# Trunk of latent and linear attention: the value and gate projections of the linear attention done as seven quadrant products a block

## The chip, the cores and the metric

The kernel runs on one core of one Trainium2 chip. The metric is device time in microseconds (us), the median of three runs. The engines are named as the profile names them: PE multiplies matrices (PEld is its weight load), DVE works on vectors, ACT evaluates activations, POOL is the general engine, SP issues DMA transfers. ACT and POOL issue transfers too.

## The reference

Two layers over 512 tokens of width 1024, all in float32. Each layer is a mixer and a squared-ReLU MLP, both with RMS norm ahead and a residual add behind. The mixer of layer 0 is latent attention (MLA), that of layer 1 gated linear attention (GLA) with four heads of key width 128 and value width 256. The part that matters:

```python
def gla_mixer(xn, w_in, w_gk_up, b_gk, g_norm, w_o):
    h = xn @ w_in                      # 1024 -> 512 q, 512 k, 1024 v, 1024 g, 16 a
    gk = log_sigmoid(a @ w_gk_up + b_gk) / 16
    # chunked scan over 64 tokens: S <- decay * S + k^T v, o = q S + (q k^T decay) v
    o = rms_norm(o, g_norm)            # per head
    o = o * silu(g)
    return o @ w_o
```

## The kernel before

The residual stream is kept transposed in SBUF: `xT[j]` is 128 channels (one eighth of the width) by 512 tokens. The program runs MLA, MLP 0, GLA, MLP 1 and the final norm.

Precision: every float32 operand of a matmul is split into a rounded high part and the remainder. `split` (L124, L127) writes the high part (`wh` for weights) on ACT and the low part (`wl`) on DVE; `piece` does this for a weight tile of 128 x 1024. `mm3` (L132 to L134) then issues three matmuls for a product: high by high, high by low, low by high. The row names of the profile that say `L132`, `L133`, `L134` are these. The two MLPs already use a scheme with seven products instead of eight (Winograd's form of Strassen), from which come the lines L917 to L920 (sums of quadrants of x), L1048 and L1056 (sums of weight quadrants), L1060 and L1064 (sums of products in PSUM).

The GLA stage has five stretches on PE: a head (first q and k projections, gate products, L1372), the blocks v and g of heads 0 and 1, the second q and k projections with the states of heads 0 and 1, the blocks V and G of heads 2 and 3, and a tail (the last head's own and past products, the turning of the gated heads, the output projection).

A block is `b_type`: 1024 input channels, 512 output columns, all 512 tokens. It takes one weight half (128 x 4 x 512) per load, cuts it in two pieces, and for each of the 8 channel groups and 4 token tiles does one `mm3` with 512 columns. The finished token tile goes to `done`: for v, `v_done` writes a high part on ACT (L1360) and a low part on DVE (L1361), with the token's norm factor `rtok`; for g, `g_done` lets ACT compute Silu (L1283), whose table is loaded ahead, with the exponential's table loaded back after (L139).

The order is set by two Python generators. `proj` yields after each piece of projection work, `heads` after each step of the recurrence; a number `PACE` times the units that `proj` yields decides how many steps of `heads` come between. The tile framework keeps each engine's instructions in program order but for priorities, and an engine waits for what its next instruction needs. `levels` is the recurrence inside chunks (L1422 to L1471); `states`, `own_tiles` and `past` build state, in-chunk and inter-chunk outputs (L1549, L1556); `gated` multiplies by the gate (L1577, L1579); `gather` turns a gated head into the layout that the output projection reads, `Y` (L149, L1598, L1599). `out_start` begins the output projection for three of its eight output groups; `out_proj` ends it. Tiles come from tagged slots: `slot("B")` is a slot of 128 x 512 of which there are few, and a slot is free only when its last reader is done.

Of the kernel before, what the change touches and what calls it, by code (L numbers as in the profile page):

```python
# [50 lines left out]
def trunk_kernel(ctx: ExitStack, tc: tile.TileContext, t_in: dict, out: bass.AP):  # L51
# [57 lines left out]

    X_AT = 44  # L110
    both_room = []
# [45 lines left out]
    W_ROOM, W_AT = 1152, 128  # L157
    AT_UP = (124, 60)

# [3 lines left out]

    def piece(raw, a, n, order=lambda i: i, at=(W_AT, W_AT)):
        hi = room_for("wh", a, n, at[0])
        lo = room_for("wl", a, n, at[1])
        split(raw, hi, lo, order=order)
        return hi, lo
# [7 lines left out]

    gains = const.tile([P, N_GAIN + NT + 32], F32, name="gains")
    pos_i = gains[:, N_GAIN : N_GAIN + NT].bitcast(I32)
    invf = gains[:, N_GAIN + NT :]


    xall = const.tile([P, ND, S], F32, name="xT")
    xT = [xall[:, j] for j in range(ND)]
    x_in = t_in["x"].rearrange("(j p) t -> p j t", p=P)

    def load_x(q, j):
        q.dma_start(xall[:, j], x_in[:, j])

    eps_t = const.tile([P, 1], F32, name="eps_t")
    DVE.memset(eps_t, EPS)  # L190
    one_t = const.tile([P, 1], F32, name="one_t")
    DVE.memset(one_t, 1.0)
    ones_r = const.tile([P, P], F32R, name="ones128")
    ones128 = f(ones_r)
    DVE.memset(ones128, 1.0)
    ident_b = rk.tile([P, P], BF16, name="ident_b")
    DVE.tensor_copy(ident_b, ident)
# [51 lines left out]
    class Norm:  # L249
# [22 lines left out]
        def scaled(self, j, src, order=lambda i: i):  # L272
            parts = self.parts[j] = both_parts(j, X_AT if self.g == "mlp" else 0)
# [3 lines left out]
            DVE.scalar_tensor_tensor(lo, src, g, f(hi), ALU.mult, ALU.subtract)  # L277
            self.out[j] = (hi, lo)
# [551 lines left out]
    def mlp(layer, nrm, nxt=None):  # L830
# [15 lines left out]
        turn = [0]  # L846
        s5 = fast.tile([P, 2 * S], F32, tag="sum", name="sum5")

        def laid(t):
# [388 lines left out]
    def gla(layer, nrm, vtag, ytag):  # L1238
# [6 lines left out]

        def b_type(c0, hf, done):
            banks = [bank("b"), bank("b"), bank("b"), bank("ac"[hf])]

            def mms(w, kk, k, t):
                xk = cut(X[k], slice(None), slice(t * P, (t + 1) * P))  # L1250
                mm3(banks[t], xk, cut(w, slice(None), kk), k == 0, k == ND - 1)

            for kc in range(2):
                raw = load(
                    w_in[kc * 512 : (kc + 1) * 512, c0 + hf * 512 : c0 + hf * 512 + 512].rearrange("(k p) n -> p k n", p=P), 4, 512
                )
                for g in range(2):
                    w = piece(raw[:, 2 * g : 2 * g + 2], 2, 512)
                    k0 = kc * 4 + g * 2
                    if k0 + 2 < ND:  # L1260
                        for kk in range(2):
                            for t in range(NT):
                                mms(w, kk, k0 + kk, t)
                            yield
                    else:
                        for t in range(NT):
                            for kk in range(2):
                                mms(w, kk, k0 + kk, t)
                            done(t, banks[t])
                            if t % 2:  # L1270
                                yield

# [3 lines left out]
        def g_done(hf):  # L1276
            G[hf] = gp.tile([P, NT, 2, HV], F32, tag="g", bufs=1, name=f"g{hf}")

            def done(t, p):
                s = G[hf][:, t]  # L1280
                with tc.high_priority():
                    tc.keep_in_program_order(
                        ACT.activation(s.rearrange("p a b -> p (a b)"), p, AF.Silu, scale=rtok[:, t : t + 1])  # L1283
                    )
                    if t == NT - 1:
                        exp_set()
                if t == NT - 1:
                    gdone.add(hf)

            return done  # L1290
# [4 lines left out]
        def proj_qk(c):  # L1295
            raw = col_chunk(w_in, c * 256, 256)
            w = [piece(raw[:, :, j * P : (j + 1) * P], ND, P) for j in range(2)]
# [25 lines left out]
        DVE.tensor_tensor(own, nrm.rstd.rearrange("p (t c) -> p t c", t=NT), ident.unsqueeze(1).to_broadcast([P, NT, P]), ALU.mult)  # L1323
        rtok = sb.tile([P, NT], F32, tag="rtok", name="rtok")
        DVE.reduce_sum(rtok, own, AX.X)


# [25 lines left out]
        vdone, gdone = set(), set()  # L1353
        V = [[None, None] for _ in range(NT)]

        def v_done(hf):
            def done(t, p):
                hi, lo = slot(vtag), slot(vtag)
                r = rtok[:, t : t + 1]
                ACT.activation(hi, p, AF.Copy, scale=r)  # L1360
                DVE.scalar_tensor_tensor(lo, p, r, f(hi), ALU.mult, ALU.subtract)  # L1361
                V[t][hf] = (hi, lo)
                if t == NT - 1:
                    vdone.add(hf)

            return done
# [161 lines left out]
        def head_values(h):  # L1528
            vs = slice((h % 2) * HV, (h % 2 + 1) * HV)
            return [cut(V[j][h // 2], slice(None), vs) for j in range(NT)]  # L1530

# [38 lines left out]
        def gated(h):  # L1570
            at, hf = AT[h], h // 2
            at["ms"] = sb.tile([P, NT], F32, tag="gms", bufs=2, name=uname("gms"))
            for i in range(NT):
                if i % 2:
                    for r in (i - 1, i):
                        sq = tmp((P, HV))
                        ACT.activation(sq, at["o"][r], AF.Square, accum_out=at["ms"][:, r : r + 1])  # L1577
                        g = G[hf][:, r, h % 2, :]
                        DVE.tensor_tensor(g, at["o"][r], g, ALU.mult)  # L1579

        def head_norm(h):
            r = small_rstd(AT[h]["ms"], NT, 1.0 / HV)
            for i in range(NT):
                g = G[h // 2][:, i, h % 2, :]
                if i % 2:
# [4 lines left out]
        def gather(h):  # L1590
            hf = h // 2
            for c in range(2):
                p = bank("c")
                for i in range(NT):
                    tr(p[:, i * P : (i + 1) * P], G[hf][:, i, h % 2, c * P : (c + 1) * P])
                hi, lo = slot(ytag), slot(ytag)
                gn = gcol("gn", 2 * layer + c)
# [4 lines left out]
        def proj():  # L1602
            parts = {
                "v": lambda: b_type(2 * DK, 0, v_done(0)),
                "g": lambda: b_type(2 * DK + D, 0, g_done(0)),
                "q": lambda: proj_qk(1),
                "k": lambda: proj_qk(3),
                "V": lambda: b_type(2 * DK, 1, v_done(1)),
                "G": lambda: b_type(2 * DK + D, 1, g_done(1)),
            }  # L1610
            for c in "vgqkVG":
                for _ in parts[c]():
                    yield 2 if c in "qk" else 1


        def heads():
            for h in (0, 2):
# [35 lines left out]
                yield from run((gather, h))  # L1653
                if h:
                    begun[0][2](4)
                yield from run((gather, h + 1))

        begun = []
        gates(0)
        for _ in rest:  # L1660
# [22 lines left out]
    load_x(ACT, 1)  # L1683
    SP.dma_start(gains, t_in["gains"])
    load_part(1, 2)
# [47 lines left out]
    psum_layout(False)  # L1733
    slot_layout(SLOT_AT)
    Y, begun = gla(0, n_mix1, "B", "B")
    n_mlp1 = Norm(ND, inv_dr, "mlp", ND)
    out_proj(t_in["gla_w_o"][0], Y, n_mlp1, begun)


# [57 lines left out]
```

## Time and profile before

| | us |
|---|---|
| median of three runs (1039.48 to 1039.76) | 1039.68 |
| profiled execution | 1039.79 |
| its span in the profile | 1038.1 |
| PE busy | 1028.9 |
| DVE busy | 879.2 |
| ACT busy | 694.4 |
| POOL busy | 92.7 |

One execution is profiled; the span runs from its first to its last instruction. The stage of linear attention takes 220.6 us of it, from 495.9 to 716.5, and the table of stretches in the prediction divides that. Rows of groups give line, engine, operation, tiles with shapes, count, then busy time and the mean of one in ns, then the engine's idle time before them with what ended it. Rows of the timeline begin with the start in us and the duration in us.

### The profile page before, as it was taken

How to read it: one execution, taken by the hardware profiler on the slowest of the kernel's cores; microseconds unless marked ns; L12 is line 12 of the kernel's file. 1: busy time of each engine (PE TensorE's matmuls, PEld its weight loads, DVE VectorE, ACT ScalarE, POOL GpSimd, SP SyncE). 2: the span in 40 equal slices, each digit the busy share in tenths (PEclk: the TensorE clock that was granted, in tenths of full speed). 3: DMA queues.
4: the chain of work that ended last, by engine and by line, in shares of the span. 5: the costliest groups of instructions: out<-in, count | busy, mean ns of one | idle time of the engine just before them, and what ended most of it. 6: DMA issues, size and time to landing. Idle time of an engine off the chain costs nothing.

```text
span 1038.1 us, 16859 instructions
## 1 busy us (share of the span) xinstructions
PE 1028.9 (99%) x6522; PEld 923.0 (89%) x6522; DVE 879.2 (85%) x1343; ACT 694.4 (67%) x1130; POOL 92.7 (9%) x128
## 2 busy tenths in 40 slices
PE   9999999999999999999999999999999999999997
PEld 7788888899999999998888888888989989989986
DVE  7889976999989989989686399469799999898994
ACT  7667754676776776786445566565677687677784
POOL 7400000400001101000000000000000001100000
PEclk9999999999999999999999999999999999999999
DMA  7501214777677777623312222164568777777422
GB/s 230 127 22 41 73 50 140 205 194 207 189 198 209 169 205 200 157 84 122 90 42 85 91 69 75 48 165 148 144 196 201 189 196 201 192 193 186 121 82 82
DMA packets 63169, 145.85 MB, mean 140 GB/s; under 512 B 9488, under 2 KB 32016, under 8 KB 60528
## 3 DMA queue, kind: packets, MB, share of 16 engines
q1 hardware_dynamic: 52928, 113.57, 33.8%
q0 software_dynamic: 8064, 29.36, 16.4%
q10 hardware_dynamic: 2096, 1.84, 0.6%
q8 instruction: 51, 0.84, 0.3%
q14 instruction: 30, 0.25, 0.1%
HBM read 142.39 MB, written 2.10 MB: 139 GB/s over the span
## 4 chain that ended last, share of the span: by engine, by line
PE 92%; DVE 4%; ACT 2%; DMA 1%; issue 1%; ACTq 0%; SPq 0%; DVEq 0%
PE ps L987 25%; PE ps L1007 13%; PE ps L1000 13%; PE ps L132 10%; PE ps L133 10%; PE ps L134 10%; PE ps L1175 2%; PE ps L149 1%; PE ps L1429 1%; PE ps L1209 1%; PE ps L436 1%; PE ps L1556 1%; DVE wl L127 1%; ACT wh L124 1%; PE ps L1479 0%
## 5 line engine op out<-in xcount | busy, mean ns | idle before, releaser
L124 ACT ACTIVATE wh<-wraw 128x1024 fp32r<-128x1024 f32 x139 | 146.1, 1056 | 113.7 <-PE ps L133 38.4
L127 DVE TENSOR_TENSOR wl<-wraw,wh 128x1024 fp32r<-128x1024 f32 x139 | 169.7, 1222 | 36.5 <-ACT wh L124 35.8
L987 PE MATMUL ps<-T,wh 128*128 128x256 f32 x896 | 154.7, 275 | 0.1
L127 DVE TENSOR_TENSOR wl<-comb,wh 128x1024 fp32r<-128x1024 f32 x112 | 136.6, 1221 | 14.4 <-ACT wh L124 14.4
L124 ACT ACTIVATE wh<-comb 128x1024 fp32r<-128x1024 f32 x112 | 118.6, 1059 | 43.3 <-issue 30.0
L987 PEld LDWEIGHTS ps<-T,wh 128*128 128x128 f32 x896 | 135.0, 188 | 0.4 <-ACT tmp L1017 0.3
L987 PE MATMUL ps<-T,wl 128*128 128x256 f32 x448 | 123.3, 275 | 0.0
L1007 PE MATMUL ps<-wh,set 128*128 128x512 f32 x392 | 122.1, 390 | 0.0
L987 PE MATMUL ps<-set,wh 128*128 128x256 f32 x672 | 116.9, 276 | 0.0
L132 PE MATMUL ps<-set,wh 128*128 128x512 f32 x280 | 109.6, 391 | 0.0
L133 PE MATMUL ps<-set,wh 128*128 128x512 f32 x280 | 109.5, 391 | 0.0
L134 PE MATMUL ps<-set,wl 128*128 128x512 f32 x280 | 109.2, 390 | 0.0
L1000 PE MATMUL ps<-hidden_parts,wh 128*128 128x256 f32 x784 | 105.8, 275 | 0.0
L987 PEld LDWEIGHTS ps<-set,wh 128*128 128x128 f32 x672 | 101.9, 188 | 0.5
L1000 PEld LDWEIGHTS ps<-hidden_parts,wh 128*128 128x128 f32 x784 | 96.6, 188 | 0.0
L987 PE MATMUL ps<-set,wl 128*128 128x256 f32 x336 | 92.5, 275 | 0.0
L1007 PEld LDWEIGHTS ps<-wh,set 128*128 128x128 f32 x392 | 73.6, 188 | 15.2
L987 PEld LDWEIGHTS ps<-T,wl 128*128 128x128 f32 x448 | 84.1, 188 | 0.0
L1007 PE MATMUL ps<-wl,set 128*128 128x512 f32 x196 | 76.3, 389 | 0.0
L987 PEld LDWEIGHTS ps<-set,wl 128*128 128x128 f32 x336 | 63.1, 188 | 0.0
L134 PEld LDWEIGHTS ps<-set,wl 128*128 128x128 f32 x280 | 52.6, 188 | 11.0
L133 PEld LDWEIGHTS ps<-set,wh 128*128 128x128 f32 x280 | 52.6, 188 | 10.9 <-DVE set L765 0.2
(406 smaller groups left out, 2189.5 us busy)
## 6 DMA issues: line engine op xcount, KB each, us to landing
comb<-in_mlp_w_down_dram SPq DMA_DIRECT2D x74, 512.0 KB, 4.2
wraw<-in_mlp_w_up_dram SPq DMA_DIRECT2D x18, 1024.0 KB, 4.9
wraw<-in_mlp_w_up_dram SPq DMA_DIRECT2D x28, 512.0 KB, 5.7
comb<-in_mlp_w_down_dram POOLq DMA_DIRECT2D x28, 512.0 KB, 7.5
wraw<-in_gla_w_in_dram SPq DMA_DIRECT2D x12, 1024.0 KB, 5.1
comb<-in_mlp_w_up_dram SPq DMA_DIRECT2D x14, 512.0 KB, 4.7
comb<-in_mlp_w_up_dram POOLq DMA_DIRECT2D x14, 512.0 KB, 6.7
wraw<-in_mlp_w_up_dram POOLq DMA_DIRECT2D x14, 512.0 KB, 7.3
```

The costliest lines, as they stand in the source:

```text
L124: order(ACT.activation(hi, src, AF.Copy))
L127: lo_eng.tensor_tensor(lo, src, f(hi), ALU.subtract)
L132: PE.matmul(psum, wh, xh, start=start, stop=False)
L133: PE.matmul(psum, wh, xl, start=False, stop=False)
L134: PE.matmul(psum, wl, xh, start=False, stop=stop)
L149: PE.transpose(psum, src, ident[: src.shape[0], : src.shape[0]])
L436: PE.matmul(p, w[:, i, j * P : (j + 1) * P], x, start=start, stop=stop)
L987: PE.matmul(o, a_, x_, start=start and j == 0 and k == 0 and n == 0, stop=k == KH - 1 and n == 2, skip_group_check=True)
L1000: PE.matmul(o, w_[:, k, j * P : (j + 1) * P], x_[:, ts], start=opens, stop=k == 1 and n == 2, skip_group_check=True)
L1007: PE.matmul(o, x_, w_, start=start and k == 0 and n == 0, stop=k == 1 and n == 2, skip_group_check=True)
L1175: PE.matmul(p, a, x, start=k == 0 and n == 0, stop=k == 3 and n == 2)
L1209: PE.matmul(o, a, b_, start=False, stop=k == 3 and n == 2, skip_group_check=True)
```

## The change

Each of the four blocks v, g, V, G is a product of x (512 tokens by 1024 channels) with a weight of 1024 by 512. The change cuts both into quadrants (256 tokens, 512 channels, 256 columns) and computes the four quadrants of the output from seven quadrant products instead of eight, as the MLPs do.

- `quadrants()` runs once at the stage's start. It makes four sums of quadrants of x (`T1` to `T4`, 16 operations of 256 elements on DVE, lines 1270 to 1273 of the changed kernel) and their high and low parts (L1290 on ACT, L1291 on DVE). T1 and T2 take the room of the residual stream in SBUF. So the eight tiles of `xT` are first copied to DRAM on POOL's queue (`kept_x`, L1259), and copied back into the same room after the last G product (`xT_back`, L1404).
- `b_type` now loads quadrants of the weight (L1303, SP). Two of the weight sums are made by a second transfer that adds to what lies in SBUF (L1305, POOL's queue); two by DVE additions of 128 x 1024 (L1344, L1355). A product is 24 matmuls of 256 columns (L1314). Partial products are copied by ACT (L1317), kept in PSUM or SBUF, and two are added on DVE (L1322). The low parts of the weight pieces of three of the seven products are computed by POOL, those of the other four by DVE.
- Values and gates come out of a block by quadrant, in halves of 256. A gate is first copied by ACT (L1390), and after the block's last product eight Silu of 256 run, with the table switched ahead and back (L1395, L139).
- The projection yields 0.7 units after each of the seven products instead of 1 after each of eight pieces of a block.
- `gather(0)` and `gather(1)` come after the last G product, and heads 0 and 1 use the slots named V there.

```diff
-        def b_type(c0, hf, done):
-            banks = [bank("b"), bank("b"), bank("b"), bank("ac"[hf])]
...
+        def quadrants():
+            for j in range(ND):
+                POOL.dma_start(kept[:, j], xall[:, j])
...
+            for k in lead:
+                g1, g2 = (gcol(nrm.g, nrm.g0 + j) for j in (k, k + KH))
+                u, v = xT[k], xT[k + KH]
+                ACT.activation(t3[k], u[:, second], AF.Copy, scale=g1)
+                DVE.scalar_tensor_tensor(t3[k], v[:, second], g2, t3[k], ALU.mult, ALU.subtract)
+                DVE.scalar_tensor_tensor(t2[k], u[:, first], g1, t3[k], ALU.mult, ALU.add)
+                DVE.scalar_tensor_tensor(t4[k], v[:, first], g2, t2[k], ALU.mult, ALU.subtract)
+                DVE.scalar_tensor_tensor(t1[k], v[:, second], g2, t2[k], ALU.mult, ALU.subtract)
...
+                    for hi, lo, x in todo:
+                        ACT.activation(hi, x, AF.Copy, scale=sign)
+                        DVE.scalar_tensor_tensor(lo, x, sign, f(hi), ALU.mult, ALU.subtract)
...
+            def fetch(base, t, plain, more=None):
+                if base is None:
+                    return
+                SP.dma_start(t, quadrant(base, *plain))
+                if more:
+                    POOL.dma_start(t, quadrant(base, *more), accum_op=ALU.add)
...
+            product(z, cut_in(a11), "11", True)
+            copied(y, z)
+            DVE.tensor_tensor(a11, s1, a11, ALU.add)
+            yield
+            product(w, cut_in(s1), "T1", True)
+            copied(w2, w)
+            fetch(c0, a22, (1, 1))
+            yield
+            product(z, cut_in(a11), "T2", False)
+            u = copied(tmp(), z)
+            yield
+            product(y, cut_in(a12, POOL), "21", False)
+            done(0, 0, y)
+            DVE.tensor_tensor(a12, a11, a12, ALU.add)
+            fetch(c_next, a11, (0, 0))
+            yield
+            p3, p22 = cut_in(s3, POOL), cut_in(a22, POOL)
+            product(z, p3, "T3", False)
+            v = copied(tmp(), z)
+            fetch(c_next, s3, (1, 1), (1, 0))
+            done(1, 1, added(w2, v))
+            yield
+            product(w, cut_in(a12), "22", False)
+            fetch(c_next, a12, (0, 1))
+            done(0, 1, added(w, u))
+            yield
+            product(z, p22, "T4", False)
+            fetch(c_next, a22, (1, 0), (0, 0))
+            done(1, 0, z)
...
+                for n, s in enumerate(G[hf][: 2 * NT]):
+                    with tc.high_priority():
+                        tc.keep_in_program_order(ACT.activation(s, s, AF.Silu, scale=rtok[:, n // 2 : n // 2 + 1]))
+                        if n == 2 * NT - 1:
+                            exp_set()
...
-                    yield 2 if c in "qk" else 1
+                    yield 2 if c in "qk" else 0.7
...
-                    yield from run((gated, 2), (own_tiles, 3), (past, 3), (gated, 3))
+                    yield from run((gather, 0), (gated, 2), (own_tiles, 3), (gather, 1), (past, 3), (gated, 3))
```

The order of the instructions moves at three places. In the head of the stage, DVE's queue around the gate product read before, from the sum over the tokens' factors to the gate operand (`tmp` of L1351; `wl` of L1335 is the low part of the gate's down weight):

```order
L1325 TENSOR_REDUCE rtok<-tmp_6029 128x4
L127 TENSOR_TENSOR wl_6143<-wraw_6140,wh_6142 128x1024
L1335 TENSOR_TENSOR wl_6035<-tmp_6033,wl_6035 128x24x16
L1312 TENSOR_TENSOR qk_6027<-ps_6001,rstd_5959 128x512
L127 TENSOR_TENSOR wl_6185<-wraw_6140,wh_6184 128x1024
L1341 TENSOR_TENSOR tmp_6045<-tmp_6038,tmp_6045 32x512
L1348 TENSOR_TENSOR tmp_6065<-ps_6048,rstd_5959 96x512
L127 TENSOR_TENSOR wl_6262<-wraw_6259,wh_6261 128x1024
L1351 TENSOR_TENSOR tmp_6067<-tmp_6065,tmp_6067 32x512
```

It reads now, from the same low part (L1453) on to the same gate operand (L1469), with `set` the parts of the x sums:

```order
L1453 TENSOR_TENSOR wl_6036<-tmp_6034,wl_6036 128x24x16
L1291 SCALAR_TENSOR_TENSOR set_6127<-set_6088,set_6127 128x256
L1291 SCALAR_TENSOR_TENSOR set_6132<-set_6089,set_6132 128x256
L1291 SCALAR_TENSOR_TENSOR set_6133<-set_6089,set_6133 128x256
L1291 SCALAR_TENSOR_TENSOR set_6138<-set_6090,set_6138 128x256
L1291 SCALAR_TENSOR_TENSOR set_6139<-set_6090,set_6139 128x256
L127 TENSOR_TENSOR wl_6219<-wraw_6210,wh_6218 128x1024
L127 TENSOR_TENSOR wl_6249<-wraw_6210,wh_6248 128x1024
L1459 TENSOR_TENSOR tmp_6046<-tmp_6039,tmp_6046 32x512
L1466 TENSOR_TENSOR tmp_6066<-ps_6049,rstd_5959 96x512
L1344 TENSOR_TENSOR wraw_6210<-wraw_6210 128x1024
L1469 TENSOR_TENSOR tmp_6068<-tmp_6066,tmp_6068 32x512
```

Between the two stand five more low parts of x sums, two weight pieces and a weight sum; the 16 sums and the other low parts stand ahead of them.

POOL's queue in the stage held the two fills of the tiles `A` between weight transfers of the MLPs:

```order
L976 DMA comb_5180<-in_mlp_w_down_dram 128x1024
L976 DMA comb_5245<-in_mlp_w_down_dram 128x1024
L1399 MEMSET A_6070 128x512
L1399 MEMSET A_6071 128x512
L976 DMA comb_8085<-in_mlp_w_up_dram 128x1024
L976 DMA comb_8094<-in_mlp_w_down_dram 128x1024
```

From the end of the saved x on (`kept_x`) it holds the accumulating transfers (L1305) and the low parts of the first two blocks (L127), in one row:

```order
L1259 DMA kept_x<-xT 128x512
L1305 DMA wraw_6211<-in_gla_w_in_dram 128x4x256
L127 TENSOR_TENSOR wl_6323<-wraw_6211,wh_6322 128x1024
L127 TENSOR_TENSOR wl_6373<-wraw_6211,wh_6372 128x1024
L127 TENSOR_TENSOR wl_6377<-wraw_6210,wh_6376 128x1024
L1305 DMA wraw_6211<-in_gla_w_in_dram 128x4x256
L1305 DMA wraw_6210<-in_gla_w_in_dram 128x4x256
L127 TENSOR_TENSOR wl_6657<-wraw_6211,wh_6656 128x1024
L127 TENSOR_TENSOR wl_6699<-wraw_6210,wh_6698 128x1024
L127 TENSOR_TENSOR wl_6703<-wraw_6211,wh_6702 128x1024
L1305 DMA wraw_7164<-in_gla_w_in_dram 128x4x256
L1305 DMA wraw_7165<-in_gla_w_in_dram 128x4x256
```

Each low part of POOL stands ahead of the transfers that fill the next block's weights.

On ACT the end of the G block was this: three Silu of 512, state parts, the fourth Silu, the table back (L1577 is the squares of head 2's output):

```order
L1549 ACTIVATE tmp_7384<-tmp_7382,D_7236 128x256 [waits DVE_49]
L1283 ACT_TABLE_LOAD
L1283 ACTIVATE g_7173<-ps_7174,rtok 128x512 [waits PE_49]
L1283 ACTIVATE g_7173<-ps_7175,rtok 128x512 [waits PE_49]
L1283 ACTIVATE g_7173<-ps_7176,rtok 128x512 [waits PE_49]
L124 ACTIVATE S_7386<-tmp_7382 128x256 [waits Activation_49]
L124 ACTIVATE S_7391<-tmp_7389 128x256 [waits DVE_49]
L1577 ACTIVATE tmp_7428,gms_7427<-ps_7331 128x256
L1283 ACTIVATE g_7173<-ps_7177,rtok 128x512 [waits PE_49]
L139 ACT_TABLE_LOAD
```

Now the last product is copied, then all eight Silu of 256 run between the two table loads, and the `kth` copies, which the states of heads 2 and 3 need, stand behind them:

```order
L1390 ACTIVATE g_7654<-ps_7490 128x256 [waits PE_49]
L1390 ACTIVATE g_7655<-ps_7490 128x256
L1395 ACT_TABLE_LOAD
L1395 ACTIVATE g_7654<-g_7654,rtok 128x256
L1395 ACTIVATE g_7654<-g_7654,rtok 128x256 [waits Activation_49]
L1395 ACTIVATE g_7654<-g_7654,rtok 128x256
L1395 ACTIVATE g_7655<-g_7655,rtok 128x256 [waits Activation_49]
L1395 ACTIVATE g_7655<-g_7655,rtok 128x256 x2
L1395 ACTIVATE g_7656<-g_7656,rtok 128x256 x2
L139 ACT_TABLE_LOAD
L124 ACTIVATE kth_7821<-ps_7817 128x384 [waits PE_49]
L124 ACTIVATE kth_7829<-ps_7825 128x384 [waits PE_49]
```

States, own tiles and past products of heads 2 and 3 so moved from inside the G block to behind it.

More of the change, by code (lines that the diff above doesn't have):

```diff
@@ L1274, in gla, with rooms @@
         G = {}
         def g_done(hf):
[L1277 to L1288, printed above, removed]
+            def rooms():
+                if hf == 0:
+                    t = gp.tile([P, 2 * NT * HV], F32, tag="g", bufs=1, name="g0")
+                    return [t[:, i * HV : (i + 1) * HV] for i in range(2 * NT)]
+                ts = [gp.tile([P, NT, 192], F32, tag="q", bufs=3, name=f"g1{i}").rearrange("p a b -> p (a b)") for i in range(3)]
+                return [t[:, i * HV : (i + 1) * HV] for t in ts for i in range(3)]
@@ new lines, in done @@
+            def done(c, th, p):
+                if hf not in G:
+                    G[hf] = rooms()
+                for i in range(2):
+                    src, dst = p[:, i * HV : (i + 1) * HV], G[hf][2 * (2 * th + i) + c]
+                    ACT.activation(dst, src, AF.Copy, scale=-1.0 if c else 1.0)
+                if (c, th) != (1, 0):
+                    return
+                for n, s in enumerate(G[hf][: 2 * NT]):
[3 more added lines that the diff above has]
+                            exp_set()
+                gdone.add(hf)
+                if hf:
+                    x = residual_room("xT_back")
+                    xT[:] = [x[:, j] for j in range(ND)]
+                    xall_of[0] = x
+                    for j in range(ND):
+                        POOL.dma_start(x[:, j], kept[:, j])
@@ L1353, in gla, with done @@
         vdone, gdone = set(), set()
[L1354 removed]
+        V = {}
         def v_done(hf):
[L1357 to L1363, printed above, removed]
+            def done(c, th, p):
+                hi, lo = V[2 * hf + c, th] = slot(vtag), slot(vtag)
+                r_all = rtok_n if c else rtok
+                for i in range(2):
+                    cs = slice(i * HV, (i + 1) * HV)
+                    r = r_all[:, 2 * th + i : 2 * th + i + 1]
+                    ACT.activation(hi[:, cs], p[:, cs], AF.Copy, scale=r)
+                    DVE.scalar_tensor_tensor(lo[:, cs], p[:, cs], r, f(hi[:, cs]), ALU.mult, ALU.subtract)
+                if (c, th) == (1, 0):
                     vdone.add(hf)
```

148 lines of the change are left out of this document (98 added, 50 removed).

## The prediction

> **What bounds the kernel now.** I read the page's busy shares first, then the chain that ended last, then busy time by stretches of the stage that the change rewrites.
>
> ```profile
> span 1038.1 us, 16859 instructions
> PE 1028.9 (99%) x6522; PEld 923.0 (89%) x6522; DVE 879.2 (85%) x1343; ACT 694.4 (67%) x1130; POOL 92.7 (9%) x128
> PE 92%; DVE 4%; ACT 2%; DMA 1%; issue 1%; ACTq 0%; SPq 0%; DVEq 0%
> 495.90:522.20 26.30, 26.30 (x116) 21.18 (x116) 16.34 (x23) 10.87 (x16) 0.53 (x1) 1.00 0.31 90
> 522.20:577.50 55.30, 55.12 (x263) 45.67 (x262) 40.23 (x94) 28.52 (x50) 0.00 (x0) 1.00 0.25 77
> 577.50:607.80 30.30, 30.30 (x168) 26.30 (x166) 18.08 (x44) 17.86 (x43) 0.00 (x0) 1.00 0.21 70
> 607.80:668.20 60.40, 60.40 (x312) 51.17 (x311) 45.38 (x102) 34.41 (x64) 0.00 (x0) 1.00 0.22 71
> 668.20:716.50 48.30, 48.28 (x231) 40.27 (x230) 36.08 (x66) 28.08 (x58) 1.72 (x2) 1.00 0.44 131
> ```
>
> The five last rows are the GLA stage: its head (gates, first q and k), the v and g blocks, the second q and k with the heads' states, the V and G blocks, the tail up to the output projection. After the window stand its length, PE, weight loads, DVE, ACT, POOL, the granted clock, the DMA share and GB/s. PE is busy for 220.4 of 220.6 us at clock 1.00: a matmul taken away is time saved, provided that no other engine lets PE wait. DVE has some 10, 15, 12, 15 and 12 us free, and POOL computes nothing in the three middle stretches.
>
> **The matmuls.** A block (one of v, g, V, G) is now 32 products with three 512-wide matmuls each.
>
> ```profile
> L132 PE MATMUL ps<-wh,set 128*128 128x512 f32 x128 | 52.4, 410 | 0.0
> L133 PE MATMUL ps<-wl,set 128*128 128x512 f32 x128 | 50.6, 395 | 0.0
> L134 PE MATMUL ps<-wh,set 128*128 128x512 f32 x128 | 50.4, 395 | 0.0
> 302.44 19.04 PE ps L1000 x168
> 799.86 19.07 PE ps L1007 x84
> ```
>
> The first three rows are all the blocks' matmuls: 384. Their durations overlap, so I take spacings from the chain, where the MLP issues the same shapes back to back: 19.07/84 = 0.227 us for 512 columns, 19.04/168 = 0.1133 us for 256. Before: 384 x 0.227 = 87.2 us. After: 4 blocks x 7 products x 24 = 672 matmuls of 256, 76.2 us. PE saves **11.1 us**, an eighth of that work.
>
> **The head.** The operands T1 to T4 are new: 16 scalar_tensor_tensor of 256, then low parts, 4 of 512 and 8 of 256. Added to them is the first weight sum (1024 wide).
>
> ```profile
> L917 DVE SCALAR_TENSOR_TENSOR comb<-xT,gains,comb x8: 472/480/486, 187.9 to 717.2; 128x256 f32<-128x256 f32 x8
> L277 DVE SCALAR_TENSOR_TENSOR set<-xT,gains,set 128x512 fp32r<-128x512 f32 x9 | 6.7, 745 | 0.0
> L1056 DVE TENSOR_TENSOR wraw<-wraw x14: 1216/1218/1223, 211.5 to 975.1; 128x1024 f32<-128x1024 f32 x14
> L1064 DVE TENSOR_TENSOR tmp<-ps,tmp x14: 682/684/684, 224.4 to 988.8; 128x512 f32<-128x512 f32 x14
> 504.72 0.69 DVE L239 SCALAR_TENSOR_TENSOR tmp<-ps,tmp 128x512 f32<-128x512 f32 x1 [3.79 <-ACT tmp L143]
> 510.62 0.55 DVE L1335 TENSOR_TENSOR wl<-tmp,wl 128x384 fp32r<-128x384 f32 x1
> 518.81 0.68 DVE L1351 TENSOR_TENSOR tmp<-tmp,tmp 32x512 fp32r<-32x512 f32 x1
> 519.71 0.40 PE L1372 MATMUL ps<-tmp,tmp 96*128 96x512 f32 x1
> ```
>
> That is 24 x 0.48 + 4 x 0.745 + 1.22 = 15.7 us by these durations, some 13.5 by spacing. DVE's free 10.0 us don't hold it, and it stands ahead of what PE needs. The gates' weight part (wl of L1335) was done at 511.2; it now stands behind the 16 sums and half of the low parts, some 4.7 us later, near 516. PE, with 81 matmuls of 0.23 ahead of them from 495.7 on, reaches its matmuls about 514.4: a stall of 1.6 us. The next order, the gate product (519.71, its operand done at 519.49), then moves by as much and finds DVE done at about 523, where PE is at 522.9. Bounds: 0, if the sums fit in DVE's idle 3.79 us before 504.72 and what follows it, and 4.5, by the longer durations with the T parts held up by the last copies of x into DRAM, into whose tile they write. I take **+2.0**.
>
> **The blocks on DVE and POOL.** Each block adds on DVE two weight sums (1.22) and two sums from PSUM (0.68): 3.80 us, 15.2 in all. V's evacuation comes in halves of 256; DVE's number of weight low parts stays at four per block, and three more go to POOL.
>
> ```profile
> L127 DVE TENSOR_TENSOR wl<-wraw,wh 128x1024 fp32r<-128x1024 f32 x32 | 39.1, 1221 | 16.2 <-ACT wh L124 16.2
> 61.12 0.28 DVE L626 TENSOR_TENSOR set<-tmp,tmp 128x128 f32<-128x128 f32 x1
> 61.77 0.71 DVE L625 TENSOR_TENSOR set<-tmp,tmp 128x128 f32<-128x128 f32 x1
> 61.56 0.78 POOL L624 TENSOR_TENSOR tmp<-set,rope_tabs_q 128x256 f32<-128x256 f32 x1 [22.47 <-DVE set L626]
> 62.67 0.56 DVE L602 SCALAR_TENSOR_TENSOR ql<-ps,qh 128x384 fp32r<-128x384 f32 x1
> 62.83 0.73 POOL L624 TENSOR_TENSOR tmp<-set,rope_tabs_q 128x256 f32<-128x256 f32 x1 [0.50 <-DVE set L626]
> 29.93 1.48 DVE L127 TENSOR_TENSOR wl<-wraw_v,wh 128x1024 fp32r<-128x1024 f32 x1
> 28.13 3.60 POOL L363 TENSOR_TENSOR rope<-rope,rope 128x128 f32<-128x128 f32 x3
> 10.18 0.46 POOL L352 TENSOR_TENSOR rope<-rope,rope 128x128 f32<-128x128 f32 x1
> ```
>
> Beside POOL a DVE addition of two SBUF tiles takes 0.71 instead of 0.28 us, one of 1024 takes 1.48 instead of 1.22; one with an input in PSUM (0.56) is not slowed. POOL loses too: 1.2 us for what takes 0.46 alone. One POOL operation of 128 elements so costs DVE 0.26 us, one of 256 0.43. For 1024 my estimate is 2.3 to 3 us of POOL time (0.46 to 0.76 is 0.3 per 128 elements), of which 8 x 0.26 = 2.1 us shut DVE out: 25 us for twelve.
> The Trainium skill (SBUF — State Buffer, "Terms" and "SBUF: two separate sides") says that DVE and GpSimd share a port pair under an exclusive lock for a whole instruction, in which the loser "fully blocks"; by it alone the twelve would cost DVE the 2.3 to 3 us in full. The rows agree on who blocks whom, and give less than the full length.
> Is there room? In the three middle stretches DVE has 103.7 us of work in 146.0. Add 15.2 and 0.7 for halves; take off some 8 that move out (states, own and past of the last two heads, as the smaller yields of 0.7 slow the heads against the products): 112. PE has 146.0 - 11.1 - 5 moved = 130. So 18 us are free. Of DVE's work about two thirds, by adding up its rows in the changed order, has two SBUF inputs, so some 17 of the 25 us block something. Room and need just match; unevenness between stretches is what PE sees. Bounds: 0 and 12 (25 - 18, and 5 for places without room). I take **+2.0**, near the lower end: POOL computes two of a block's three parts some products ahead of their use.
> ACT gains per block three copies of 1024 and four of 512 (5.5 us), and more for G's halves; with 28.5 and 34.4 us busy now it stays below PE.
>
> **DMA.** Weight sums are made by accumulating transfers on POOL's queue.
>
> ```profile
> wraw<-in_mlp_w_up_dram POOLq DMA_DIRECT2D x14, 512.0 KB, 7.3
> wraw<-in_gla_w_in_dram SPq DMA_DIRECT2D x12, 1024.0 KB, 5.1
> ```
>
> Plain load and accumulation in a row take 5 + 7 = 12 us; a block of products takes 168 x 0.1133 = 19 us with the heads' work between. Each fetch is issued four products or more ahead: taken as nothing; if POOL's low part ahead of them in its queue comes late, 3 us a block. x goes out in eight 256 KB transfers and comes back during the tail, wanted first by the residual add some 20 us after: nothing.
>
> **The tail.** Here a cover is lost. In the kernel of before the sigmoid table and the gate's Silu ran while PE had V, G and ready output products.
>
> ```profile
> 664.69 1.28 ACT L1283 ACT_TABLE_LOAD   x1
> 665.98 1.84 ACT L1283 ACTIVATE g<-ps,rtok 128x512 f32<-128x512 f32 x3
> 669.40 1.28 ACT L139 ACT_TABLE_LOAD   x1
> 668.20 0.40 PE L1556 MATMUL ps<-set,ADh 128*128 128x256 f32 x2
> 670.69 0.40 PE L132 MATMUL ps<-set,wh 128*128 128x512 f32 x1
> ```
>
> PE went from its last G matmul at once to the last head's own and past, and at 670.69 to output products of the first two heads. Now those two heads are turned only after G, and states, own and past of heads 2 and 3 lie there too. On ACT, after the last product (time P), stand two copies (0.7), the table (1.28), eight Silus of 256 (2.8, by half of 1.84/3 and a little), the table back (1.28): only at P+6 come the two kth copies (0.5 each) that the states need. PE has own tiles and turns, 24 x 0.1133 and 0.8 = 3.5 us, up to there: 3 us idle. Then eight small ACT steps (0.4 each) stand ahead of the first turned head; it is ready about P+12, and PE has some 3.7 us of work in those 5.5. Sum 3 + 1.8 = 4.8; bounds 2 and 7. I take **+4.5**, as DVE may let ACT run a little ahead.
>
> **Sum.** 1039.79 (profiled: span 1038.1 and 1.7 around it; the median 1039.68 is 0.1 lower) - 11.1 + 2.0 + 2.0 + 4.5 = 1037.2, **1037 us**, 0.25% faster. I count 0.2% (2.1 us) as the bound of what can be told from no change.
>
> **Rivals.**
> A, *POOL's operations hold DVE up* (the other side): at the low parts of a block DVE waits for POOL, PE for DVE. For it: 25 us of held time against 18 free, and the 0.71 for 0.28. Against: the idle DVE of 15 us in each block pair. Price 8 to 12 on PE instead of 2: 1043 to 1047. It decides from 6.7 us on, 0.56 us of PE for each POOL operation. Chance 0.26.
> The Trainium skill's whole-instruction lock (SBUF — State Buffer, "SBUF: two separate sides"), held in full for 12 x 2.6 = 31 us, would give an estimate of about 1049.
> B, *the losses just eat the gain*: head 3, blocks 3 to 4, tail 5: 1040. The change then does nothing. 0.20.
> C, *the covers hold*: head 0.5, blocks 0, tail 3: 1032. For it: PE's queue is fixed, but every operand is ready well ahead in the trace of before. 0.20.
> D, *late sums from DRAM*, 3 us in two or more blocks on top of the forecast: 1043 to 1048. Against: DMA share of 0.21 to 0.25 there. 0.08.
> The forecast itself (1035 to 1038.5): 0.26.
>
> **Numbers.** Faster by over 0.2%: C and most of the forecast, 0.43. Within: B and the rest, 0.21. Slower: A, D and a little of B, 0.36. The likeliest's own range is 1034 to 1040; since both signs hold much, the range goes from C less some to A with most of its price: 1030 to 1049.
>
> **What would show it.** Right: products of 256 at 0.113; in the head one wait of PE for DVE of 1 to 3 us before the 96-row gate matmuls; PE waits in the blocks of 2 us together; 3 to 6 us of PE idle within 13 us of the last G product, released by ACT. Wrong: PE waiting for wl tiles of POOL or DVE by more than 6 us in v to G, POOL's 1024-wide operation well above 3 us, DVE's low parts far above 1.22 beside it; PE waiting for DMA at the third or fifth product.

## The result and the profile after

The changed kernel takes 1070.57 us in the median of four runs (1069.8 to 1071.81) against 1039.58 us for the kernel before on the same chip: slower by a ratio of 1.03 (95% interval 1.0282 to 1.0318), 31 us. I had forecast 1037 with a range of 1030 to 1049. The page of its profiled execution, first its span, busy times and chain, then the granted clock in the 40 slices:

```profile
span 1069.5 us, 17680 instructions
PE 1033.5 (97%) x6810; PEld 940.1 (88%) x6810; DVE 923.9 (86%) x1395; ACT 726.3 (68%) x1206; POOL 142.8 (13%) x164
PE 78%; DVE 11%; ACT 6%; issue 3%; DMA 2%; POOL 0%; SPq 0%; ACTq 0%; DVEq 0%; POOLq 0%
PEclk9999999999999999999988998999999999999999
```

PE's share of the chain fell from 92 to 78%, DVE's rose from 4 to 11, and the clock has dents that it did not have. The same stretches of the stage as before (head in two rows, v and g, q and k, V and G, tail; the next MLP starts about 748):

```profile
490.45:516.00 25.55, 24.55 (x107) 19.82 (x107) 25.55 (x50) 17.51 (x33) 5.91 (x8) 1.00 0.69 168
516.00:524.00 8.00, 7.97 (x35) 5.83 (x34) 7.43 (x11) 2.48 (x4) 0.00 (x0) 1.00 0.09 22
524.00:584.00 60.00, 51.22 (x372) 50.09 (x371) 50.33 (x100) 33.68 (x60) 18.11 (x8) 0.89 0.40 103
584.00:612.00 28.00, 27.50 (x163) 23.88 (x163) 14.53 (x21) 17.94 (x35) 2.58 (x2) 1.00 0.58 132
612.00:682.60 70.60, 60.31 (x428) 56.85 (x428) 63.66 (x127) 42.66 (x93) 21.99 (x16) 0.93 0.41 112
682.60:748.00 65.40, 59.47 (x299) 50.54 (x299) 45.34 (x85) 41.49 (x87) 1.75 (x2) 0.95 0.38 114
```

Two windows of 10 us out of v and g, in which DVE (the third number behind the length) is full:

```profile
550.00:560.00 10.00, 10.00 (x81) 10.00 (x80) 9.95 (x30) 4.35 (x9) 0.00 (x0) 1.00 0.01 2
560.00:570.00 10.00, 6.71 (x36) 5.77 (x36) 10.00 (x18) 4.92 (x9) 5.64 (x2) 0.75 0.09 21
```

PE is without work for 1.0 us in the head, 8.8 in v and g, 0.5 in q and k, 10.3 in V and G, 5.9 in the tail, and its clock is 0.89, 0.93 and 0.95 where it waits most. From the starts of the matmuls (spacing less 0.113 or 0.227 us) I get 30.2 us in gaps of more than 0.4 us (0.5 before), and 15.2 us lost in matmuls that come at over 1.6 times their spacing (3.3 before). The gaps add up to more than the 26.5 us of the table because a matmul's recorded 0.28 us reach into the gap behind it. So 29.7 us of idle and 11.9 us of slow matmuls, less the 11.1 us saved, make 30.5 of the 31.4 us by which the span grew.

What PE waits for in the stage, by the view of waits (engine and line, for whom, total us, times, longest). In the changed kernel L1549 are the in-chunk products, L1314 the block products, L1463 the gates' first product, and L132 with `kth` the states of heads 2 and 3:

```profile
PE ps L1549 <- ACT q L1556: 7.9, 3, 5.5
PE ps L132 <- ACT kth L124: 5.4, 2, 4.9
PE ps L1314 <- DVE wl L127: 3.7, 3, 1.9
PE ps L1549 <- DVE q L1575: 2.3, 1, 2.3
PE ps L1314 <- ACT wh L124: 2.3, 4, 0.7
PE ps L1314 <- DVE g L1698: 2.0, 1, 2.0
PE ps L1463 <- DVE wl L1453: 1.0, 1, 1.0
```

Behind the first row stands DVE. The timeline there, and at two more places, of DVE and POOL:

```profile
527.39 1.23 DVE L1355 TENSOR_TENSOR wraw<-wraw,wraw 128x1024 f32<-128x1024 f32 x1 [1.81 <-POOL wl L127]
529.22 4.97 POOL L127 TENSOR_TENSOR wl<-wraw,wh 128x1024 fp32r<-128x1024 f32 x2 [1.86 <-DVE T L1502]
529.79 2.15 DVE L1510 TENSOR_TENSOR T<-T 128x256 f32<-128x256 f32 x1
531.86 2.88 DVE L1502 TENSOR_TENSOR T<-tmp,tmp 128x512 f32<-128x512 f32 x1
538.78 2.93 PE L1549 MATMUL ps<-q,qk 128*128 128x192 f32 x8 [5.49 <-ACT q L1556]
564.36 5.66 POOL L127 TENSOR_TENSOR wl<-wraw,wh 128x1024 fp32r<-128x1024 f32 x2 [24.43 <-DVE A L1584]
564.55 3.23 DVE L127 TENSOR_TENSOR wl<-wraw,wh 128x1024 fp32r<-128x1024 f32 x1
567.85 2.72 DVE L1542 TENSOR_TENSOR qk<-qk,T 128x512 f32<-128x512 f32 x1
620.64 2.33 DVE L312 TENSOR_TENSOR sm<-sm,sm 128x4 f32<-128x4 f32 x1
```

A DVE step of 4 elements takes 2.33 us, one of 256 takes 2.15, one of 512 takes 2.88 (0.16, 0.42 and 0.69 in the kernel before): each beside a POOL subtraction of 2.4 to 2.7 us. I call this a hold. The gate's scan (L1502, L1510), which the first in-chunk products wait for, met two of them in a row. The longest holds lengthen one DVE step by some 2 us; adding up the means of the lengthened groups gives about 20 us for the twelve, 1.7 us each.

POOL costs DVE a second thing, the first row: the weight sum of L1355 overwrites a tile that POOL still reads, so DVE stood 1.81 us until POOL was done, ahead of the same scan.

### The profile page after: what moved, and what is told of

Read it like the earlier page. It is cut to its first block, busy times and chain, and to the rows that moved or that the text cites. A ratio compares the mean times of both kernels' runs of the same rounds, so it can differ in the third digit from the quotient of the medians.

```text
span 1069.5 us, 17680 instructions
## 1 busy us (share of the span) xinstructions
PE 1033.5 (97%) x6810; PEld 940.1 (88%) x6810; DVE 923.9 (86%) x1395; ACT 726.3 (68%) x1206; POOL 142.8 (13%) x164
## 4 chain that ended last, share of the span: by engine, by line
PE 78%; DVE 11%; ACT 6%; issue 3%; DMA 2%; POOL 0%; SPq 0%; ACTq 0%; DVEq 0%; POOLq 0%
PE ps L992 24%; PE ps L1012 12%; PE ps L1005 12%; PE ps L132 6%; PE ps L133 6%; PE ps L134 6%; PE ps L1314 3%; DVE wl L127 2%; PE ps L1180 2%; PE ps L149 1%; PE ps L1214 1%; ACT wh L124 1%; DVE qk L1542 1%; PE ps L440 1%; DMA wraw<-in_gla_w_o_dram 1%
## 5 line engine op out<-in xcount | busy, mean ns | idle before, releaser
L124 ACT ACTIVATE wh<-wraw 128x1024 fp32r<-128x1024 f32 x151 | 158.4, 1055 | 96.4 <-issue 38.4
L127 DVE TENSOR_TENSOR wl<-wraw,wh 128x1024 fp32r<-128x1024 f32 x139 | 173.3, 1249 | 29.3 <-ACT wh L124 28.5
L127 DVE TENSOR_TENSOR wl<-comb,wh 128x1024 fp32r<-128x1024 f32 x112 | 136.6, 1221 | 14.4 <-ACT wh L124 14.4
L132 PE MATMUL ps<-set,wh 128*128 128x512 f32 x280 | 109.8, 392 | 0.2 <-ACT set L1717 0.2
L1012 PEld LDWEIGHTS ps<-wh,set 128*128 128x128 f32 x392 | 73.6, 188 | 15.2
L1314 PE MATMUL ps<-wh,set 128*128 128x256 f32 x320 | 62.6, 289 | 1.1 <-ACT wh L124 1.1
L992 PEld LDWEIGHTS ps<-set,wl 128*128 128x128 f32 x336 | 63.1, 188 | 0.0
L132 PEld LDWEIGHTS ps<-set,wh 128*128 128x128 f32 x280 | 52.6, 188 | 11.1 <-ACT set L1717 0.4
```

The lines of the kernel that those rows point to most:

```text
L124: order(ACT.activation(hi, src, AF.Copy))
L127: lo_eng.tensor_tensor(lo, src, f(hi), ALU.subtract)
L132: PE.matmul(psum, wh, xh, start=start, stop=False)
L992: PE.matmul(o, a_, x_, start=start and j == 0 and k == 0 and n == 0, stop=k == KH - 1 and n == 2, skip_group_check=True)
L1012: PE.matmul(o, x_, w_, start=start and k == 0 and n == 0, stop=k == 1 and n == 2, skip_group_check=True)
L1314: PE.matmul(p, x_, w_[:, k], start=start and t == 0 and k == 0 and n == 0, stop=k == KH - 1 and n == 2, skip_group_check=True)
```

## The experiments

Ratios are against the kernel before, with their 95% interval.

**Where the low parts are computed.** All on DVE:

```diff
-            product(y, cut_in(a12, POOL), "21", False)
+            product(y, cut_in(a12), "21", False)
-            p3, p22 = cut_in(s3, POOL), cut_in(a22, POOL)
+            p3, p22 = cut_in(s3), cut_in(a22)
```

> The changed kernel with one edit: all seven low parts of a block are computed by DVE, none by POOL. Theory P (the port): each of the twelve POOL subtractions shuts DVE out for about 2.1 us (3.23 instead of 1.22 us for a low part beside one), DVE does the same work itself in 1.13 us, so DVE gains some 11.6 us in stretches where it is busy all the time, PE idles less and keeps its clock: 1052 to 1062 us. Theory L (DVE's load and its order are the cause, POOL is a help): DVE has 13.6 us more to do where it is the bound: 1075 to 1090 us.

1059.5 us, 1.0193 (1.0176 to 1.021): 11 us faster than with POOL. DVE's mean for a low part is 1222 ns and for the 512-wide group 689, so the holds are gone, and DVE is busy for 915.0 us in place of 923.9 although it does twelve operations more. DVE, which I had thought relieved by POOL, is better off with the work itself. But 20 us against the kernel before are left with no subtraction on POOL at all.

POOL writing instead of subtracting:

```diff
-        lo_eng.tensor_tensor(lo, src, f(hi), ALU.subtract)
+        if lo_eng is POOL:
+            POOL.memset(f(lo), 0.0)
+        else:
+            lo_eng.tensor_tensor(lo, src, f(hi), ALU.subtract)
```

> The changed kernel, but POOL's twelve operations of 128x1024 write zeros into the low parts of these weights instead of reading weight and high part and subtracting, so three products of a block lack the low part of the weights; the operations, their waits and their places stay. Theory P: without reads from SBUF POOL shuts DVE out little or not at all, no DVE row beside it is longer than alone, and the time falls by most of what the holds cost: 1040 to 1052 us. Theory L: the time stays, 1066 to 1072 us.

1046.98 us, 1.0075 (1.006 to 1.0091): 23.6 us came back, and DVE is busy for 903.1 us, 20.8 less. DVE's groups, with POOL subtracting and with POOL writing (mean ns after the busy time):

```profile
L127 DVE TENSOR_TENSOR wl<-wraw,wh 128x1024 fp32r<-128x1024 f32 x24 | 33.2, 1388 | 8.9 <-ACT wh L124 8.8
L1542 DVE TENSOR_TENSOR qk<-qk,T 128x512 f32<-128x512 f32 x28 | 23.1, 829 | 0.9 <-ACT E L1591 0.9
```

```profile
L130 DVE TENSOR_TENSOR wl<-wraw,wh 128x1024 fp32r<-128x1024 f32 x24 | 29.2, 1222 | 10.9 <-ACT wh L124 10.6
L1545 DVE TENSOR_TENSOR qk<-qk,T 128x512 f32<-128x512 f32 x28 | 19.2, 688 | 1.9 <-ACT E L1594 1.9
```

Without POOL's reads the means are those of the kernel before (1221 and 685). What PE waits in all for ACT's operands of the in-chunk products, 7.9 us in the changed kernel, is all but gone:

```profile
PE ps L1552 <- ACT q L1559: 0.3, 1, 0.3
```

The edit took away one thing more than I had expected. A zero write reads nothing, so it waits neither for the weight nor for its high part and begins earlier, and DVE's weight sum no longer waits for POOL to have read a tile. A POOL write takes 0.95 us and a subtraction 2.43, so the length differed too. Three writes in a row, 2.9 us, answer that:

> As the run in which POOL writes zeros, but three such writes of 128x1024 for each of the twelve (about 2.9 us, longer than a subtraction of 2.43), so only the reading of SBUF is left out, not POOL's time. Three products of a block lack the weights' low part. If POOL's reading beside DVE's is what holds DVE up, the time stays within 3 us of the single write: 1046 to 1050 us, and no DVE row beside POOL is longer than alone. If POOL's length or its late results are what cost, it goes back toward the changed kernel: 1060 to 1070 us.

1051.17 us, 1.0122 (1.0105 to 1.0139), a little above the range: DVE's two groups have means of 1222 and 684 ns. So no hold; PE's gaps in the stage are 4 us longer than with one write, and I did not find out which result of POOL they wait for. Of the 23.6 us about 19 belong to POOL's reading, the holds and the waits for its inputs and readers together; these two runs do not part them. In the changed kernel PE waited for no tile of POOL, and DVE once, the 1.81 us above.

The opposite test: the kernel before, three of the four low parts of a block on POOL, nothing else (`lo_eng=POOL if kc or g else DVE` at its `piece`).

> The kernel before with one edit: three of the four weight low parts of a block go from DVE to POOL, twelve in all, nothing else. Theory P: twelve holds of some 2.1 us against 13.6 us that DVE no longer does; DVE rows beside POOL near 3.2 us; DVE had 42 us free in these stretches, so the cost in time is 0 to 6 us: 1040 to 1046. Theory L: DVE has less to do, POOL is not in the way: 1038.5 to 1040.

1050.01 us, 1.0105 (1.0085 to 1.0126): 10.8 us slower, more than theory P said, though DVE had 13.6 us less to do. This kernel has no weight sums in these blocks and PE waits for no tile of POOL, so the holds stand here alone. DVE's costliest group, of 685 ns before, and one of POOL's subtractions:

```profile
L1422 DVE TENSOR_TENSOR qk<-qk,T 128x512 f32<-128x512 f32 x28 | 27.2, 976 | 1.5 <-ACT E L1471 1.5
541.87 2.38 POOL L127 TENSOR_TENSOR wl<-wraw,wh 128x1024 fp32r<-128x1024 f32 x1 [15.59 <-ACT wh L124]
```

Here the room on DVE was certain, 42 us, and the holds still reached PE.

Shorter holds: each POOL subtraction in eight of 128x128.

> The changed kernel, with each POOL subtraction of 128x1024 cut into eight of 128x128; nothing left out. If POOL holds DVE off for the length of one instruction and lets it in between, no DVE row beside POOL is lengthened by more than 0.3 to 0.5 us at a time, but POOL takes longer for a piece (8 x 0.46 and DVE's turns between, 6 to 12 us), so the low parts come later: 1066 to 1078 us. If instead the single long hold at a bad place (2.15 us for a step of 0.4) was what cost, the time falls to 1055 to 1062.

1068.89 us, 1.0276 (1.0258 to 1.0295), as the first theory said. The long holds are gone (the low parts' mean is 1260 ns, the 512-wide group's 755; DVE is busy for 912.1 us), and the time is not: POOL's operation of 128 elements takes 0.64 us on the mean, a piece so 3.4 to 5.8 us. The 13 small steps of the first scan, all beside POOL now, take 4.15 us in place of 2.04, so PE's first gap stays (5.2 us). And DVE's weight sums wait longer for POOL, 7.1 us in all:

```profile
L1361 DVE TENSOR_TENSOR wraw<-wraw,wraw 128x1024 f32<-128x1024 f32 x4 | 5.4, 1345 | 7.1 <-POOL wl L131 7.1
```

Neither form pays.

**DVE's load.** The weight sums left out, with POOL writing zeros:

> The run with one zero write by POOL, and besides the two weight sums of a block that DVE computes (1.22 us each) are left out, so two products use weights that are not summed: DVE has 9.8 us less in the four blocks. If DVE's load is what still makes PE wait in the blocks (about 5 us of idle and as much of slower clock), 4 to 8 us come back: 1039 to 1043 us. If it is latency of single steps, 0 to 3 us: 1044 to 1047.

1048.46 us, 1.0082 (1.0065 to 1.0099), above both ranges, with an interval that overlaps that of the single write: nothing came back from 9.8 us less of DVE work. With these twelve low parts made by nobody, DVE's load is not the bound in the blocks. That their remaining gaps are latencies of single steps is what is left, and no run shows it. With the twelve on DVE (1059.5 us) 12.5 us more are lost than with nobody making them, so there DVE's work does count.

**The products and the layout.** Eight plain quadrant products (in place of seven, four raw quadrants, no sums); in this kernel two weight quadrants stand in each other's place, which changes values and not the work.

> The changed kernel with eight plain quadrant products a block in place of seven: no sums of x or of weights, no accumulating transfers, four weight low parts a block, all on DVE, none on POOL. Quadrant layout, halves of 256, copies of x, Silu at the end and the order of the turned heads stay as changed, and the yields add up to the same. Theory P: PE's 11 us come back, but without holds and with less for DVE the blocks wait no more; what is left against before is the tail: 1043 to 1048 us. If the layout or the slower heads alone cost much, it stays above 1055.

1045.22 us, 1.0055 (1.0038 to 1.0072). With 96 matmuls more than the seven products PE has one gap of over 0.4 us in the stage, 3.8 us, in the tail:

```profile
PE ps L132 <- ACT kth L124: 3.6, 1, 3.6
```

This is what theory P expected. So layout and tail cost about 6 us, and the seven products with their POOL parts another 25 instead of saving 11.

**The order.** Heads pushed on faster, `yield 2 if c in "qk" else 8 / 7`:

> The changed kernel, with 8/7 units a product instead of 0.7, so that a block of seven products pushes the heads on as far as the eight pieces of before did. A third theory O (the order): the slower heads leave their work to places where nothing covers it; then the time falls by 8 us or more, to 1062 or less, above all behind the last G product. Theories P and L: DVE's sum is unchanged, the time stays within 4 us, 1066 to 1075, and waits only change place.

1076.85 us, 1.0364 (1.0343 to 1.0384): slower by 6, against theory O and outside what the others said. PE now stands 7.8 us for the copy of a turned head, 0.2 in the changed kernel:

```profile
PE ps L132 <- ACT set L1717: 7.8, 1, 7.8
```

So the slow pace alone does not explain the loss.

**The tail.** The last block's Silu deferred: they are no longer issued in `done` but as a step behind the states, `run((gather, 0), (silus, 1), (gated, 2), ...)`.

> The changed kernel with one edit: the eight Silu of the last block, with their two table loads, are issued behind the states of heads 2 and 3 instead of right behind the block's last copies, so the kth copies no longer stand behind them. If the tail's idle of PE (0.8 + 5.1 us there, and some 2 us of slower clock behind it) is due to that queue on ACT, 4 to 7 us come back: 1063 to 1067 us. If the tail waits for something else just as late (the late load of the output weights, DVE's backlog), the time stays within 2 us of 1070.

1071.17 us, 1.0306 (1.0291 to 1.0322): no gain. The tail of the changed kernel on ACT, as forecast, with the kth copies behind the table and the Silu:

```profile
686.87 1.28 ACT L1395 ACT_TABLE_LOAD   x1
688.16 3.30 ACT L1395 ACTIVATE g<-g,rtok 128x256 f32<-128x256 f32 x8
691.48 1.28 ACT L139 ACT_TABLE_LOAD   x1
692.77 0.87 ACT L124 ACTIVATE kth<-ps 128x384 fp32r<-128x384 f32 x2
```

PE's waits with the deferred Silu:

```profile
PE ps L132 <- ACT kth L124: 3.5, 2, 3.0
PE ps L132 <- ACT set L1721: 3.1, 1, 3.1
```

The first wait is shorter and a new one has come: the turned heads' copies (`set`) now stand behind the same Silu. The burst needs 6 us on ACT, and in neither place is enough ready on PE to cover it.

With both edits, low parts on DVE and the Silu deferred:

> Both edits together: all seven low parts on DVE and the last block's Silu behind the states. If the two losses are separate, the gains add up: 1059.5 less 4 to 7, 1052 to 1056 us. If the late Silu only uncovers DVE's backlog, it stays at 1058 to 1060.

1060.76 us, 1.0207 (1.0186 to 1.0227), no better than DVE alone. Then the Silu behind the turning of both first heads, `run((gather, 0), (gather, 1), (silus, 1), (gated, 2), (own_tiles, 3), (past, 3), (gated, 3))`, with eight products:

> Eight plain quadrant products a block, and the last block's Silu behind the states and behind the turning of both first heads, with the output projection's first products to cover them. If the queue on ACT is what the tail loses (3.8 us of idle and the clock behind it in the run with eight products), the time comes near the kernel before: 1039 to 1042 us. If the tail waits elsewhere, 1044 to 1046.

1043.48 us, 1.0039 (1.0025 to 1.0054), between the two expectations and 1.7 less than with the Silu at the block's end, though the two intervals overlap; and with seven products and POOL writing zeros once:

> POOL writes zeros once in place of each subtraction (three products of a block lack the weights' low part), and the last block's Silu is issued behind the states and behind the turning of both first heads. If what the change loses is the sum of POOL's reading, the tail's queue on ACT and slower clock, nearly all of it is gone: 1040 to 1044 us, and PE's idle in the blocks (about 5 us) with its clock is what still stands against the 11.1 us of saved matmuls. If the tail's loss belongs to something else, 1046 to 1048.

1044.98 us, 1.0053 (1.0035 to 1.0071). Two microseconds came back against the single write with the Silu at the block's end (the intervals just overlap), between the two expectations, and the time stays above the kernel before, although three low parts a block were free. So no version with seven products that I ran beats it, and none of these points to one.

**The clock.** Unused matmuls in PE's gap from 533.3 to 538.8:

```diff
+                        for _ in range(46):
+                            PE.matmul(p, quad["11"][0][:, 0, :P], quad["11"][1][:, 0], start=True, stop=True)
```

> The changed kernel with 46 matmuls of 256 columns, whose results nobody uses, ahead of the first in-chunk product of head 0, where PE sat idle for 5.5 us; they take 5.2 us. If the idle itself is what slows the clock afterwards (0.21 us instead of 0.113 for 256 columns during some 5.7 us), the matmuls behind it run at 0.113 and 2 to 3 us come back: 1067 to 1069 us. If the slow clock there has another cause (load, heat of the stage), the spacing stays at 0.21 and the time at 1070 to 1071.5.

1069.32 us, 1.0288 (1.0273 to 1.0303); its interval overlaps that of the changed kernel, so the time alone settles little (the span of the profiled execution is 1066.6 us against 1069.5). The spacing settles it. PE's rows behind the gap, changed kernel first, then with the fill:

```profile
542.58 0.63 PE L1314 MATMUL ps<-wh,set 128*128 128x256 f32 x2
543.00 0.41 PE L1314 MATMUL ps<-wl,set 128*128 128x256 f32 x1
543.22 0.63 PE L1314 MATMUL ps<-wh,set 128*128 128x256 f32 x2
```

```profile
540.51 0.39 PE L1315 MATMUL ps<-wh,set 128*128 128x256 f32 x2
540.74 0.28 PE L1315 MATMUL ps<-wl,set 128*128 128x256 f32 x1
540.85 0.39 PE L1315 MATMUL ps<-wh,set 128*128 128x256 f32 x2
```

Three matmuls take 0.64 us after the idle and 0.34 with the fill. So it is the idle itself that slows what follows here.

## Why the prediction was wrong

- *The matmuls, 11.1 us.* Right as a count: the products run at 0.113 us where the clock is 1.00.
- *The head, 2.0.* Right in place, half in size: PE waits 1.0 us for the gate's low part (the L1463 row above); the gate product behind it waits for nothing that counts.
- *The holds.* The prediction gave 25 us of held time and 17 of it felt. POOL's operation took 2.56 us on the mean, and DVE lost about 20 us: the size was nearly right. That DVE also has to wait until POOL has read a tile, 1.81 us ahead of the first scan, stood in no term.
- *The cover, "room and need just match", 2.0, bound 12.* This is the step that failed. 18 us of free time, averaged over 130 us, was set against holds that fall at fixed places. DVE was full for whole stretches (9.95 and 10.00 of 10 us from 550 on, in the two windows of 10 us shown with the result), and its chain from gate to in-chunk product has no room. The two block stretches lose 19.1 us of idle, not 2; with POOL's reads out of the way, the stage has 12.5 us of idle in gaps and not 30.2, so most of what POOL's reading cost DVE came out at PE. Even the kernel before, with more room (42 us) and less work on DVE, lost 10.8 us to the same holds. The upper bound, 25 - 18 = 7 and 5 more, rested on the same average. The sign that I had set, PE waiting over 6 us for low parts, would have missed it: by name that wait is 3.7 us, and the rest shows as waits for the operands of the in-chunk products (7.9 and 2.3), behind which DVE's held steps stand.
- *The clock.* It stood in no term. I read 1.00 in every window of before and priced idle at its own length. 11.9 us of slow matmuls were added, near 0.4 us for each of idle. Of the 34 us between the forecast and the profiled execution (1071.2) the cover makes 17 and the clock 12. The Trainium skill (TensorE: Matmul & The Clock Gate, "Part 1: The HAM clock gate (the "warmup" mystery)") says that PE falls to half its clock after an idle window of about 3.4 us and needs as long a busy one to return. The gap of 5.5 us and the 0.213 for 0.113 us behind it agree; the return took some 5.7 us here, and gaps of at most 2.2 us, close together, were followed by slow matmuls too (last section). I had not used it.
- *The tail, 4.5.* Right in its mechanism and in its idle time: ACT's queue from the last product's copy to the kth copies took 6.6 us (forecast 6), and PE idled 5.1 us there and 0.8 ahead of it. But ACT began it only 2.7 us after the product had ended (683.5), behind a weight piece and two more steps, so kth came at P+9.2 and not at P+6; and with the slow matmuls behind the gap, some 3.7 us more than before, the tail lost over 9 us, above its bound of 7.
- *Rival A* named the mechanism, with 8 to 12 us as its price. Its time (1043 to 1047) was short for the same two reasons, cover and clock. I gave it 0.26, as much as the forecast itself. The whole-instruction lock of the Trainium skill (SBUF — State Buffer, "SBUF: two separate sides") fits the longest holds, 2.1 us and more on DVE for an operation of 2.43, and my estimate by it, 1049, was short too.
- *DMA.* Right for the accumulating transfers: neither PE nor ACT nor DVE waited for one by name. A late load of the output weights held ACT for 1.4 us at the end of the G block, just ahead of the tail's queue.

Not settled: how the 19 us divide between the holds and DVE's waits for POOL, and what the blocks still lose without POOL's reads (about 5 us of idle). The latter is not DVE's load (the run without weight sums), and I did not take the steps apart further.

## What to carry to other kernels

Before you move elementwise work from DVE to POOL, look for a row where both run: here a subtraction of 1024 cost DVE 1.7 us on the mean, and 2.2 at the worst, when POOL did it and 1.13 when DVE did. Look also for tiles that DVE writes again after POOL has read them. Do not set an average of free time against such holds; ask which chain each one meets, and add the clock, since PE ran at half speed for some 6 us after a wait of 5.5. A scheme that saves matmuls pays only while PE is the one that is waited for: an eighth less of the products, 11.1 us, was outweighed nearly four times.

## What was not expected of the hardware

- POOL's writes alone (0.95 us for 128x1024) do not slow DVE: means of 1222 and 684 ns in the run with three writes in place of each subtraction.
- A DVE operation with one SBUF tile and a per-partition factor is held too: two steps of L1707 (128x256) took 2.85 us together, 0.62 for the next two.
- PE's clock falls after several short gaps as well: gaps of 1.0, 0.8, 0.4 and 2.2 us between 562.4 and 567.8 were followed by slow matmuls until 571.8 (granted clock 0.50 from 568 to 571), one of 2.1 us alone at 621 was not (1.00).
